# Another fixed instruction order for the engines of a hybrid SSM and attention layer, up to its first FFN tiles

## The chip, the cores and the metric

The kernel runs on one core of one Trainium2 chip. The time is the device time of one execution in microseconds; the time before is the median of three runs, 641.48 (640.93 to 643.57).

## What is computed

One layer of a hybrid encoder runs over 512 prompt tokens and 64 sample tokens (a running stream with 256 past keys), all in float32. Cut to what matters:

```python
def hybrid_layer(x, ckv_past, krope_past, ssm_h0, conv_buf, p):
    proj = rmsnorm(x, p['norm_mix']) @ p['w_in']        # z, xbc, dt, cq, ckv
    xbc, conv_new = causal_conv(xbc, conv_buf, p['conv_w'], p['conv_b'])
    dt = softplus(dt_raw + p['dt_bias'])
    y, h_new = ssd_scan(xh, dt, A, Bm, Cm, ssm_h0)      # chunks of tokens
    y_ssd = rmsnorm((y + d_skip * xh) * silu(z), p['ssd_norm'])
    q = rmsnorm(cq, p['q_norm']) @ p['w_uq']            # 8 heads: 64 + 32 rotary
    o = attention(q, keys)                              # mask in chunks of 64
    x = x + concat([y_ssd, o], -1) @ p['w_out']
    hf = rmsnorm(x, p['norm_ffn'])
    x = x + (silu(hf @ p['w_gate']) * (hf @ p['w_up'])) @ p['w_down']
```

A final norm follows. The new keys, the SSM state and the conv state are outputs too.

## The kernel before

The 576 tokens stand along the free axis, in two halves of 288; channels stand on the partitions in tiles of 128. A large product keeps its precision by splitting: a weight tile arrives by a DMA on SyncE's queue (`weights`, L119, 128 x 1024 floats, 512 KB, into one of seven slots of a pool), ScalarE casts it to its high part (L112, `wh_`) and VectorE subtracts to get the low part (L113, `wl_`). The operands are split in the same way (L142 on ScalarE, L144 or L146 on VectorE). Every product is then three passes, high by high, high by low, low by high (L128, and L443 for one half of the tokens at a time).

The stages, in the order in which the program is written:

- First: the first products (L128, `ps_first`, weights loaded at L213 and split at L217 and L218), their norms, and the small product `ps_small` (L292). The latter writes two 48-row results into two halves of the array's columns.
- Conv tiles 0 to 7 (`conv_tile`): a product into `ps_in` (L128, two PSUM buffers), its evacuation to `up` on VectorE (L382 to L384), the four-tap convolution (L389 on ScalarE, L391 three times on VectorE), a tanh (L393) and the result (L395, L396) into `xsd` or `bc`. Between them lies the step-size chain on VectorE (`sp_a`, L348 to L353), a run of small operations of 128 x 40, which starts from a transposition into `ps_dt` (L335).
- The rotary queries (`q_rope`): `ps_qr` (L128), then products with cosine and sine on VectorE (L421, L422 and L423, tiles `rrp` and `qt`). The PSUM pools of these stages are then closed, and their banks go to the next stages.
- z tiles (`ps_z`, L443, evacuated at L453), and the SSD scan in five chunks: `chunk_a` turns x and B (`ps_x` L483, `ps_b` L491), `chunk_e` builds the decays E (L506 to L514), `chunk_b` makes the outputs (`ps_y`, L527, and `ps_i`, L538), `chunk_s` the state (`ps_s`, L548), `gate` the gating and its norm (L567 to L573, `ps_g` L572).
- Values of the latent keys (`ps_v`, L590), and for each of four head pairs p: `pair_proj` (`ps_q` and `ps_k`, L443), scores of four query blocks and of the sample tokens (`sc` L657, `sc_s` L663), the softmax (`pr`, L640 to L647), turning (`ptp` L679, `ptp_s` L687), values (`pv` L704, and `pvs` L715 for the sample tokens), and splitting of the result (`cat`, L696 and L697).
- The output product in tiles of its own (`ps_o`, L443), then the FFN: `ps_p`, `ps_x`, `ps_y` and `ps_z` (L852), and `ps_d` (L988 and L1050).

Five of these matmuls fill only half of the array's columns, because their output has 48 or 64 rows for each head or half: L292, L527, L663, L704 and L715. Two that stand side by side write the two halves of one bank. This is L704's loop (L527 and L715 look alike):

```python
    for b in range(4):
        for j in range(2):
            h = 2 * p + j
            pe.matmul(
                pv[64 * j : 64 * j + 64, b * P :], V[b][:, h * HD : (h + 1) * HD], pts[p, b, j],
                start=b == 0, stop=True, skip_group_check=b > 0,
            )
```

The order of each engine's instructions is not the order of the program. After all of it is written, `issue_in_order` (L1296) takes, engine by engine, the list `ISSUE` of places: number n stands for the n-th instruction that the program gave this engine. Each instruction gets a dependency on the one ahead of it in the list, so each engine issues in just this order. The five lists are those of TensorE (PE), VectorE (DVE), ScalarE (ACT), GpSimd (POOL) and SyncE (SP); SyncE's and GpSimd's hold the DMAs that they issue.

Of the kernel before, what the change touches and what calls it, by code (L numbers as in the profile page):

```python
# [1295 lines left out]
def issue_in_order(tc, nc):  # L1296
# [13 lines left out]
0-7 20-21 8 14-16 9-13 22-25 38-41 17-19 32-36 26-31 42-43 56-59 37 50-55 68-69 44-47 60-61 74-79 92 48-49 62-67 80-85  # L1310
98-99 93-97 70-73 86-91 104-106 100-103 110 107-109 122-126 134-135 111-115 128-133 148-153 116-121 136-141 127
142-147 154-169 174-175 170-171 270-274 176-221 172-173 222-269 275-370 373-420 371 421-468 372 469-634 637 641-644
638-640 657-660 635-636 665-697 661 698-718 662 737-758 719-720 663-664 721-726 763 645-652 759-760 727-736 764-766
653-656 767-768 771-794 769-770 795-818 859 761-762 819-826 860-861 833-836 862-864 837-840 827-832 865-870 841-845
871-872 846-852 873-874 853-856 875-877 880 878-879 857-858 881-887 904-911 888 912 892-899 889-891 900-903 925-926
913-921 927-935 922-924 939-940 936-938 949-957 964-966 941 945-948 967 958-963 968-969 942-944 970-975 987 976-979
1003 980-986 991-993 988 1004-1005 1015-1021 1006-1014 1022-1024 994-996 1025-1026 1029-1034 1043-1045 997-998 989
1000-1002 999 1046-1054 990 1035-1039 1059-1061 1040-1042 1062-1064 1027-1028 1075-1077 1081-1092 1055-1056 1078-1080
1057 1093-1096 1058 1097-1104 1121-1123 1071-1072 1124-1129 1065 1068-1070 1073 1105-1107 1066-1067 1074 1130-1143
1119 1144-1156 1120 1229-1232 1157 1108-1112 1233-1240 1113-1114 1158 1241-1245 1115-1118 1159-1161 1246-1247 1176  # L1320
1253-1262 1177 1248-1252 1263-1264 1162-1175 1180 1178 1181-1182 1265 1183 1266-1268 1277-1278 1179 1279 1184-1187
1190-1195 1269-1275 1196-1204 1188-1189 1205-1223 1276 1227-1228 1224-1226 1280-1297 1301-1303 1298-1300 1304-1321
1342-1343 1348-1355 1344-1347 1322-1341 1356-1511 1572 1512-1559 1575-1576 1560-1571 1577 1596-1598 1578 1573-1574
1593 1584-1585 1579 1581-1583 1602-1604 1623-1625 1594-1595 1614 1586 1605-1606 1590-1592 1611-1613 1632-1634
1587-1589 1608-1610 1607 1580 1599-1601 1620-1622 1641 1626-1628 1647-1648 1629-1631 1649 1642-1643 1615-1616
1635-1637 1617-1619 1638-1640 1653 1656 1658-1667 1644-1646 1650-1652 1654-1655 1668-1669 1657 1682 1694-1705
1683-1693 1670-1681 1730-1741 1706-1729 1742-1748 1754-1755 1749-1753 1756-1767 1778-1785 1768-1777 1786-1885
1898-1905 1886-1897 1906-2017 2030-2036 2018-2029 2037-2053 2066-2084 2054-2065 2085-2089 2102-2104 2090-2101
2105-2221 2234-2236 2240-2241 2222-2233 2237 2242-2248 2238-2239 2249-2725 2738-2740 2744 2726-2737 2741 2745-2751
2742-2743 2752-3229 3242-3244 3248 3230-3241 3245 3249-3255 3246-3247 3256-3733 3746-3748 3752 3734-3745 3749  # L1330
3753-3759 3750-3751 3760-4189
""",
    "DVE": """
1 0 2-3 48 4-5 7 6 9 12 8 10-11 13-15 17 16 18-20 23 21-22 49 24 58 25 30 26 85 27-29 31-34 67-68 106 36 69 108 37 105
35 38 107 70 44 94 71 39 109 72-73 40-41 74 50-52 110 42 75 82 112 53 43 54-55 59-61 76 121 45 77-79 62 80 63-64 86-88
81 57 65 56 89 66 83 90 130 91 95 84 96-97 46 98-100 113-114 103 115 47 139 116 93 117 92 111 118 122-123 148 124
101-102 125 120 126-127 119 131-133 155 134 129 135-136 140-142 149 152 128 170 143-144 138 104 150 145 153 147 151
154 156 137 146 174 157 178 159 171-172 187 169 160 158 161-162 176 206 163 175 183 180 164 167 165-166 168 215 181
177 188 173 189 182 184 190 195 191 179 192-194 197 185-186 224 196 204 207-209 198-203 214 205 210 288 211 225
216-218 212 220 222 219 213 226 221 223 227-228 233 229 234 230-232 235-236 245 255 246 237 294 256 247 239 248 257  # L1340
259 258 260 240 238 264 241 261 242 263 262 307 267 243 265 244 266 274 249 268 270 251 269 253 250 252 254 275-276
289 271 290 277-279 295 286 280 282 281 287 272 297 317 291 283 318 273 298 302 299 316 300 284-285 319 303 306
292-293 296 309 312 304 326 305 310 308 313 327 362 311 328 322 301 323 314 363 330 324 320 329 315 336 321 325 364
333 367 337 331-332 365 340 338 334-335 341 344 349 339 345 350 342 346 352 351 343 355 358 366 347 359 357 348 360
356 353 361 368 377 354 370-371 369 372 375-376 373-374 382 390 378 384 383 385-386 379 389 387 380 397 388 381 393
405 395 391 396 398 394 392 400 399 401 403 402 420 406 404 408 407 409 412 410 417 414 411 413 418 462 416 421 423
419 464 425 422 424 415 433 431 426 432 429 428 427 438 430 434 469 463 436 435 437 439 442 441 443 466 440 444 451
465 446 467-468 452-453 445 447 455 454 448 473 475 456 477 476 474 457 472 470 478 458-459 449-450 479 460 481 480
461 471 482 491 487 483 496-497 484 488 498-499 489 500-502 485-486 503 510 490 515-518 522 492 504 519 506 520 507
521 508 532-535 539 546 493-495 536 547-549 505 511-512 509 523 537 529-530 524-525 513-514 531 538 540 528 550 541  # L1350
566 526 542 527 551 543 545 552 544 567-568 553-554 569 555 574 570 556-559 561 575-576 560 565 577 562 578-581 571
582-583 572 563 590-591 584 592 585-586 564 598 573 599-600 593-594 587-588 601 589 603 602 595 604-607 596 610 597
608-609 620-623 611 627 612 624 613-614 625-626 619 634-636 628 637 617 638 618 629 616 615 630 641 639 631 640 633
632 654-656 642 657 643 662 658 644-647 649 663-664 648 653 665 650 666-669 659 670-671 660 651 678-679 672 680
673-674 652 686 661 687-688 681-682 675-676 689 677 691 690 683 692-695 684 698 685 696-697 708-711 699 715 700 712
701-702 713-714 707 722-724 716 725 705 726 706 717 704 703 718 729 727 719 728 721 720 742-744 730 745 731 750 746
732-735 737 751-752 736 741 753 738 754-757 747 758-759 748 739 766-767 760 768 761-762 740 774 749 775-776 769-770
763-764 777 765 779 778 771 780-783 772 786 773 784-785 796-799 787 803 788 800 789-790 801-802 795 810-812 804 813
793 814 794 805 792 791 806 817 815 807 816 809 808 830-832 818 833 819 839 834 820-823 825 840-841 824 829 842 826
843-846 835 847-848 836 827 855-856 849 857 850-851 828 864 837 865-866 858 838 859 852-853 867 854 869 868 860  # L1360
870-873 861 876 862 874 880 875 881-883 887 884 863 885 877 886 879 878 888-898
""",
    "ACT": """
0-5 8 6-7 10 9 13 11 14 12 15 17-18 16 21 19 24 20 23 40 22 25 44 26-27 51 28-33 48-49 55 34-35 37 36 59 50 41-42
38-39 63 43 45-47 52-53 67 54 56-57 71 58 60-61 75 62 64-66 76 68-70 72 91 73-74 93 78 87 77 80 103 81 89 83 115 85-86
102 84 82 99 97 79 96 88 98 101 100 95 90 125 104 92 110 108-109 155 114 94 106-107 112 121 113 111 141 116 162 105
117-118 135 126 136 133 127 139 134 123 120 119 138 128 137 140 129 122 142 130 124 149 145 148 131 209 132 144 147
153 151 150 146 157-158 156 143 154 159-161 152 163-164 211 169 171 170 165 167 179 185 168 180 173 186 174 172 175
188 166 189 176 226 177 191 178 192 187 181 194 193 190 182 199 195 183-184 198 200 196 212 207 214-215 201-202 218
208 203 216 233 217 197 204-205 210 213 225 219 232 220 239 206 222 241 223 221 240 228 242-243 224 270 234 229 227  # L1370
230 237 236 271 231 244 235 247 238 245 248-251 246 256 254 260 253 261 255 258 262 257 264 252 266 265 263 267-268
277 269 259 272-276 283 279-281 284 286 282 278 292 285 290 287 289 288 301 291 293 295 294 297 299 296 300 302-303
# [123 lines left out]
```

## Time and profile before

| | |
|---|---|
| median of 3 runs | 641.48 us (640.93 to 643.57) |
| the profiled execution | 639.76 us, of which the span of its instructions is 638.1 |
| granted TensorE clock | 0.998 |
| stages, as windows of the span (us) | conv tiles 16 to 85; q_rope, z and SSD 85 to 149; attention 149 to 222; output product and first FFN tiles 222 to 306; rest of the FFN and the end from 306 |

A row of the timeline reads: start in us, length in us, engine, line, operation, output and inputs, array rows by columns used, shape, count in the group; in brackets the idle time before it and who ended it. Consecutive matmuls overlap, since the next one begins while the one before drains, so the cost of one is read from start to start. A plain float32 matmul counts as two records in the trace (x2), an fp32r pass as one. In a windows row stand start and end, length, and then for PE, PEld (weight loads), DVE, ACT and POOL the busy us with the number of instructions, the granted clock, the DMA share and GB/s. Numbers behind a tile's name tell its copies apart, and the profile leaves them out.

### The profile page before, as it was taken

To read this page: it belongs to the slowest core of one execution; us is meant where nothing else is said; L and a number is where in the kernel's file an instruction comes from. 1 tells how busy PE (TensorE), PEld (TensorE's weight loads), DVE (VectorE), ACT (ScalarE), POOL (GpSimd) and SP (SyncE) were. 2 spreads that over 40 slices of the span, in tenths; PEclk is the share of its full clock that TensorE was granted. 3 is DMA by queue.
4 is the path that set the end of the run, shared out by engine and by line. 5 is a ranking of instruction groups with operands and counts; after the bars stand their busy time and mean duration, and the time that the engine had idled before them with its cause. 6 is when DMAs were issued, how large, how long until landed. Compare 5 with 4: busy or idle time off the path is not lost.

```text
span 638.1 us, 12090 instructions
## 1 busy us (share of the span) xinstructions
PE 627.0 (98%) x4635; PEld 598.9 (94%) x4635; DVE 543.5 (85%) x945; ACT 400.9 (63%) x768; POOL 110.4 (17%) x164
## 2 busy tenths in 40 slices
PE   9999999999999999999999999999999999999996
PEld 8899999986787799999999999999999999999995
DVE  6999986899876699999999888988899789986555
ACT  7645436778775567766566676566757665767364
POOL 1322103101010000001300330033103220323323
PEclk9999999999999999999999999999999999999999
DMA  9322366322231133235643986398737892589914
GB/s 320 130 61 71 97 158 159 108 80 60 87 123 61 56 111 102 89 116 183 239 141 101 205 185 153 82 186 194 169 100 156 197 206 100 101 211 258 259 27 148
DMA packets 39593, 89.19 MB, mean 140 GB/s; under 512 B 4570, under 2 KB 14312, under 8 KB 39280
## 3 DMA queue, kind: packets, MB, share of 16 engines
q1 hardware_dynamic: 26416, 63.12, 30.5%
q0 software_dynamic: 12400, 24.73, 20.9%
q8 instruction: 36, 0.59, 0.4%
q10 hardware_dynamic: 720, 0.57, 0.3%
q14 instruction: 21, 0.17, 0.1%
HBM read 62.74 MB, written 24.53 MB: 137 GB/s over the span
## 4 chain that ended last, share of the span: by engine, by line
PE 84%; DVE 3%; ACT 1%; issue 1%; POOL 1%; DMA 1%; POOLq 0%; DVEq 0%; ACTq 0%
PE ps_x L852 21%; PE ps_d L1050 14%; PE ps_z L852 11%; PE ps_o L443 8%; PE ps_y L852 5%; PE ps_in L128 4%; PE ps_z L443 3%; PE ps_l L988 3%; PE ps_d L988 2%; PE ps_p L852 2%; PE sc L657 2%; PE pv L704 2%; PE ptp L679 1%; PE ps_v L590 1%; PE ps_q L443 1%
## 5 line engine op out<-in xcount | busy, mean ns | idle before, releaser
L852 PE MATMUL ps_x<-xop,wh_gu_S 128*128 128x288 f32 x504 | 101.7, 295 | 0.0
L852 PEld LDWEIGHTS ps_x<-xop,wh_gu_S 128*128 128x128 f32 x504 | 80.7, 188 | 0.2
L852 PE MATMUL ps_x<-xop,wl_gu_S 128*128 128x288 f32 x252 | 74.0, 294 | 0.0
L113 DVE TENSOR_TENSOR wl_gu_S<-gu,wh_gu_S 128x1024 fp32r<-128x1024 f32 x44 | 53.4, 1221 | 10.3 <-ACT wh_gu_S L112 6.8
L1064 POOL DMA_DIRECT2D acc<-fz x32 | 27.9, 907 | 167.2 <-ACT fz L1061 138.3
L112 ACT CAST wh_gu_S<-gu 128x1024 fp32r<-128x1024 f32 x44 | 46.3, 1052 | 15.9 <-PE ps_y L852 8.2
L852 PEld LDWEIGHTS ps_x<-xop,wl_gu_S 128*128 128x128 f32 x252 | 47.3, 188 | 0.0
L128 PE MATMUL ps_in<-xs,wh_in 128*128 128x288 f32 x256 | 45.3, 298 | 0.8 <-DVE sp_a L351 0.6
L128 PEld LDWEIGHTS ps_in<-xs,wh_in 128*128 128x128 f32 x256 | 37.6, 189 | 1.9 <-issue 0.9
L852 PE MATMUL ps_z<-xop,gu_a 128*128 128x288 f32 x252 | 38.3, 295 | 0.0
L852 PEld LDWEIGHTS ps_z<-xop,gu_a 128*128 128x128 f32 x252 | 35.0, 188 | 0.0
L852 PE MATMUL ps_z<-xop,wh_gu_S 128*128 128x288 f32 x168 | 34.9, 297 | 0.0
L852 PE MATMUL ps_x<-xop,wh_gu_A 128*128 128x288 f32 x168 | 34.6, 297 | 0.0
L852 PE MATMUL ps_y<-xop,wh_gu_A 128*128 128x288 f32 x168 | 33.9, 294 | 0.0
L112 ACT CAST wh_gu_A<-gu 128x1024 fp32r<-128x1024 f32 x22 | 23.1, 1051 | 10.4 <-PE ps_x L852 7.0
L443 PE MATMUL ps_o<-cat_y,wh_out 128*128 128x288 f32 x128 | 29.3, 312 | 0.4 <-ACT cat_y L142 0.4
L113 DVE TENSOR_TENSOR wl_gu_A<-gu,wh_gu_A 128x1024 fp32r<-128x1024 f32 x22 | 26.8, 1220 | 1.4 <-ACT wh_gu_A L112 1.0
L852 PEld LDWEIGHTS ps_z<-xop,wh_gu_S 128*128 128x128 f32 x168 | 27.2, 189 | 0.3 <-ACT wh_gu_S L112 0.3
L128 PE MATMUL ps_in<-xs,wl_in 128*128 128x288 f32 x128 | 27.4, 296 | 0.0
L852 PEld LDWEIGHTS ps_x<-xop,wh_gu_A 128*128 128x128 f32 x168 | 27.2, 189 | 0.1
L852 PEld LDWEIGHTS ps_y<-xop,wh_gu_A 128*128 128x128 f32 x168 | 26.9, 188 | 0.0
L443 PE MATMUL ps_z<-xs,wh_z 128*128 128x288 f32 x128 | 26.4, 299 | 0.0
(384 smaller groups left out, 2012.0 us busy)
## 6 DMA issues: line engine op xcount, KB each, us to landing
gu<-in_w_gu SPq DMA_DIRECT2D x44, 512.0 KB, 5.3
wr_d<-in_w_down SPq DMA_DIRECT2D x18, 512.0 KB, 4.1
acc<-fz POOLq DMA_DIRECT2D x16, 288.0 KB, 6.6
acc<-da POOLq DMA_DIRECT2D x16, 288.0 KB, 7.8
acc<-dc POOLq DMA_DIRECT2D x16, 288.0 KB, 8.4
wr_in<-in_w_in SPq DMA_DIRECT2D x8, 512.0 KB, 3.8
wr_out<-in_w_out SPq DMA_DIRECT2D x8, 512.0 KB, 3.2
cumb<-cumD SPq DMA_DIRECT2D x5, 512.0 KB, 4.6
```

Of the source, the lines that this page charges most:

```text
L112: act.copy(hi, raw)
L113: dve.tensor_tensor(lo, raw, hi.bitcast(F32), ALU.subtract)
L128: pe.matmul(ps[:m, hf, :n], w, x[:, hf * n : (hf + 1) * n], start=start and k == 0 and i == 0, stop=stop and k == last and i == 2,)
L443: pe.matmul(ps[:, :n], w, x[:, cols], start=k == 0 and i == 0, stop=k == len(terms) - 1 and i == 2,)
L590: pe.matmul(ps[:n], l, r, start=j == 0, stop=j == 2)
L657: pe.matmul(s[:, :nk], qs[:, j, q0 : q0 + P], ks[:, j, :nk], start=True, stop=True)
L679: pe.transpose(pp[:, k : k + P], prs[p, i][:, j, b * P : b * P + P], ident)
L704: pe.matmul(pv[64 * j : 64 * j + 64, b * P :], V[b][:, h * HD : (h + 1) * HD], pts[p, b, j], start=b == 0, stop=True, skip_group_check=b > 0,)
L852: pe.matmul(ps, p, q, start=not onto and first and kp == kps[0] and j == 0, stop=onto or (last and kp == kps[-1] and j == 2), skip_group_c ...
L988: pe.matmul(ps, w, x[:, cols], start=first and k == 0 and i == 0, stop=last and k == len(terms) - 1 and i == 2,)
L1050: pe.matmul(ps, p, v, start=not onto and n == 0 and j == 0, stop=onto or (n == len(ks) - 1 and j == 2), skip_group_check=onto,)
L1064: pool.dma_start(out, src, accum_op=ALU.add)
```

## The change

All five lists of `ISSUE` are replaced by others. In every list the places are the same numbers, so no instruction is added, removed or given other operands. TensorE's list is the same as before from place 1922 on, which lies in the first FFN tiles.

```diff
 ISSUE = {
     "PE": """
-0-7 20-21 8 14-16 9-13 22-25 38-41 17-19 32-36 26-31 42-43 56-59 37 50-55 68-69 44-47 60-61 74-79 92 48-49 62-67 80-85
...
+0-7 20-21 8 14-16 9-10 22 11-13 23-25 38-39 26-31 17-19 32-33 40 34-36 41-43 56 37 50-55 44-45 57-61 68-69 46-49 62-65
...
```

The numbers tell a reader nothing, so here are three places as rows of the two orders. The first is on TensorE, where head pair 0's values are computed (L704 `pv`, L715 `pvs`), with the next pairs' `ps_q` and `ps_k` (L443) about them. Before, from the scores that stand ahead of the values:

```order
L657 MATMUL sc_1_1_2075<-ks_385,qs_384 128x256
L704 MATMUL pv_2172<-pt_0_2035,V_1659 64x512 x2
L704 MATMUL pv_2172<-pt_1_2098,V_1659 64x384 x2
L704 MATMUL pv_2172<-pt_2_2087,V_1670 64x256
L715 MATMUL pvs_2233<-pts_2052,V_1681 64x64 x3
L704 MATMUL pv_2172<-pt_2_2087,V_1670 64x256
L704 MATMUL pv_2172<-pt_2_2087,V_1670 64x128 x2
L715 MATMUL pvs_2233<-pts_2052,V_1681 64x64
L715 MATMUL pvs_2233<-pts_2052,V_1692 64x64 x2
L663 MATMUL sc_s<-ks_385,qs_384 64x320 x2
L443 MATMUL ps_q_0_2287<-cqn_481,wh_pair_2244 128x288 x2
L443 MATMUL ps_q_0_2287<-cqn_481,wl_pair_2245 128x288
```

And now, from the first of the values:

```order
L704 MATMUL pv_2172<-pt_0_2035,V_1659 64x512
L657 MATMUL sc_1_1_2075<-ks_385,qs_384 128x256
L704 MATMUL pv_2172<-pt_0_2035,V_1659 64x512
L704 MATMUL pv_2172<-pt_1_2098,V_1659 64x384
L663 MATMUL sc_s<-ks_385,qs_384 64x320
L715 MATMUL pvs_2233<-pts_2052,V_1681 64x64
L443 MATMUL ps_q_1_2196<-cqn_481,wh_pair_2155 128x288 x2
L443 MATMUL ps_q_1_2196<-cqn_481,wl_pair_2156 128x288
L443 MATMUL ps_q_1_2196<-cqn_484,wh_pair_2155 128x288 x2
L443 MATMUL ps_q_1_2196<-cqn_484,wl_pair_2156 128x288
L715 MATMUL pvs_2233<-pts_2052,V_1681 64x64 x3
L663 MATMUL sc_s<-ks_385,qs_384 64x320
```

What stood in one run behind each other, the eight values of the prompt, the sample's and the scores of the next sample block, is now dealt out among full-width products; the remaining values of this pair follow in the same manner, in four more pieces.

The second place is on VectorE, in the conv tiles: the step-size chain (`sp_a`, L350 to L353), the evacuations (L382 to L384), the weight splits (L113) and the copy of the keys (L313). Before:

```order
L384 TENSOR_TENSOR up_631<-ps_in_582,R_99 128x64
L350 SCALAR_TENSOR_TENSOR sp_a<-sp_a,sp_q 128x40
L113 TENSOR_TENSOR wl_in_914<-wr_in_911,wh_in_913 128x1024
L313 TENSOR_TENSOR ckv<-ckf,ckv 128x832
L350 SCALAR_TENSOR_TENSOR sp_a<-sp_a,sp_q 128x40 x3
L391 SCALAR_TENSOR_TENSOR cacc_639<-up_631,hcw,cacc_639 128x579
L350 SCALAR_TENSOR_TENSOR sp_a<-sp_a,sp_q 128x40
L391 SCALAR_TENSOR_TENSOR cacc_639<-up_631,hcw,cacc_639 128x579 x2
L382 TENSOR_TENSOR up_732<-ps_in_683,R_99 128x288
L383 TENSOR_TENSOR up_732<-ps_in_683,R_99 128x224
L384 TENSOR_TENSOR up_732<-ps_in_683,R_99 128x64
L351 SCALAR_TENSOR_TENSOR sp_a<-sp_a,sp_s 128x40
```

And now, up to the end of the chain:

```order
L352 TENSOR_SCALAR dt<-dt 128x40
L350 SCALAR_TENSOR_TENSOR sp_a<-sp_a,sp_q 128x40 x2
L391 SCALAR_TENSOR_TENSOR cacc_567<-up_559,hcw,cacc_567 128x579
L310 SCALAR_TENSOR_TENSOR ckf<-ckr,par,Rk 128x576
L391 SCALAR_TENSOR_TENSOR cacc_567<-up_559,hcw,cacc_567 128x579 x2
L382 TENSOR_TENSOR up_631<-ps_in_582,R_99 128x288
L383 TENSOR_TENSOR up_631<-ps_in_582,R_99 128x224
L384 TENSOR_TENSOR up_631<-ps_in_582,R_99 128x64
L396 SCALAR_TENSOR_TENSOR xsd<-cth_572,cacc_567 128x64
L395 SCALAR_TENSOR_TENSOR xsd<-cth_572,cacc_567 128x512
L351 SCALAR_TENSOR_TENSOR sp_a<-sp_a,sp_s 128x40
L353 SCALAR_TENSOR_TENSOR dt<-sp_a,dt 128x40
```

The chain is now at its end before the second evacuation's tile is convolved, and the split of `wr_in_914` and the copy L313 no longer stand between the chain's steps; they come later.

The third place is on VectorE at the rotary queries (L421 to L423). Before:

```order
L421 TENSOR_TENSOR rrp<-ps_qr_1133,cos_sin 128x576 x2
L395 SCALAR_TENSOR_TENSOR xsd<-cth_979,cacc_974 128x512
L113 TENSOR_TENSOR wl_z_1324<-wr_z_1321,wh_z_1323 128x1024
L391 SCALAR_TENSOR_TENSOR cacc_1118<-up_1110,hcw,cacc_1118 128x579 x2
L396 SCALAR_TENSOR_TENSOR bc<-cth_1051,cacc_1046 128x64
L362 TENSOR_SCALAR ncum<-ps_cum 128x40
L422 TENSOR_TENSOR qt_419<-ps_qr_1146,cos_sin 128x576
L391 SCALAR_TENSOR_TENSOR cacc_1118<-up_1110,hcw,cacc_1118 128x579
L422 TENSOR_TENSOR qt_420<-ps_qr_1146,cos_sin 128x576
L396 SCALAR_TENSOR_TENSOR bc<-cth_1123,cacc_1118 128x64
```

And now:

```order
L421 TENSOR_TENSOR rrp<-ps_qr_1133,cos_sin 128x576 x2
L391 SCALAR_TENSOR_TENSOR cacc_1118<-up_1110,hcw,cacc_1118 128x579
L422 TENSOR_TENSOR qt_419<-ps_qr_1146,cos_sin 128x576
L391 SCALAR_TENSOR_TENSOR cacc_1118<-up_1110,hcw,cacc_1118 128x579
L422 TENSOR_TENSOR qt_420<-ps_qr_1146,cos_sin 128x576
L391 SCALAR_TENSOR_TENSOR cacc_1118<-up_1110,hcw,cacc_1118 128x579
L423 TENSOR_TENSOR rrp<-rrp,qt_419 128x576
L423 TENSOR_TENSOR rrp<-rrp,qt_420 128x576
L396 SCALAR_TENSOR_TENSOR bc<-cth_1123,cacc_1118 128x64
L113 TENSOR_TENSOR wl_z_1324<-wr_z_1321,wh_z_1323 128x1024
```

The split of the z weights 1324 stood ahead of the L422 products; it now stands behind them and behind L423. SyncE's queue moves too: the first conv weights (`wr_in_504`) are now issued ahead of four of the eight first-product weights (L213), and the loads of the chunks' decays (L473, L479) and of `ks_385` (L603) change places with the z and pair weights.

More of the change, by code (lines that the diff above doesn't have):

```diff
@@ new lines @@
+391-420 371 421-468 372 469-500 517-520 501-507 521-522 508 523 509-516 524-595 613-617 596-608 618-621 637 641
+609-610 622-632 611-612 633-636 642 638-640 665-672 689-696 673-681 697-705 682-688 706-712 643-644 713-717 657 718
+737-752 658 753 659-662 645-647 754-755 653 756-757 648-649 719-725 654 726-727 758-759 650-651 760 652 728-736
+655-656 771-774 795-797 775-776 663 763-764 664 777-783 765-767 798-799 784-794 800-818 761-762 819-824 768-770
+825-826 833-835 859-860 836-839 861-864 840 827-832 865-867 841-842 845-854 868-872 880-881 873 855-856 843-844
@@ new lines @@
+1293-1296 1288 1297-1299 1301-1307 1300 1308-1329 1342 1330-1332 1348-1355 1333-1341 1356 1343-1347 1357-1377
+1380-1382 1378-1379 1383-1426 1428-1429 1427 1430-1504 1572 1505-1511 1575 1512-1515 1581 1516-1522 1578 1523
+1579-1580 1584-1585 1524-1547 1573-1574 1593 1548-1553 1599-1600 1554-1557 1560-1563 1558 1564-1566 1594 1567-1570
+1559 1571 1582-1583 1602 1595 1614 1601 1576-1577 1596-1597 1590 1587-1589 1620 1608-1609 1591-1592 1610 1629
+1615-1616 1635 1621 1586 1605-1607 1598 1617-1619 1603-1604 1623-1625 1644 1611-1612 1630 1613 1631 1650 1632-1634
@@ new lines @@
+1653 1638 1626 1636-1637 1622 1656 1639-1640 1658-1659 1651 1645-1646 1654 1627-1628 1647 1660-1662 1655 1663-1668
+1641-1643 1648-1649 1657 1682 1694-1705 1669 1683-1684 1652 1685-1693 1670-1680 1730-1732 1681 1733-1739 1706-1729
+1742-1750 1766-1767 1740-1741 1751 1778-1788 1752-1765 1768-1776 1790-1791 1777 1792-1813 1789 1826-1828 1832-1834
+1838-1840 1844-1846 1814-1825 1829-1831 1841-1842 1850-1852 1843 1853-1858 1862-1863 1868-1869 1864-1865 1870
+1835-1837 1847-1849 1859-1861 1866 1871-1872 1867 1874-1885 1898-1908 1886-1887 1909 1888-1897 1910-1921 1873
```

147 lines of the change are left out of this document (71 added, 76 removed).

## The prediction

> **What bounds the kernel now.** I read the page first: which engine is full, and which engine the last chain runs through. The third row gives the size and the landing time of one kind of weight load.
>
> ```profile
> PE 627.0 (98%) x4635; PEld 598.9 (94%) x4635; DVE 543.5 (85%) x945; ACT 400.9 (63%) x768; POOL 110.4 (17%) x164
> ...
> PE 84%; DVE 3%; ACT 1%; issue 1%; POOL 1%; DMA 1%; POOLq 0%; DVEq 0%; ACTq 0%
> ...
> wr_in<-in_w_in SPq DMA_DIRECT2D x8, 512.0 KB, 3.8
> ```
>
> TensorE is busy for 98% of 638.1 us, so all waits together hold about 11 us, start and end included. A new order gains only what it takes out of those waits, and loses whatever it makes TensorE itself do more slowly. The second view is the list of TensorE's waits (total, times, longest).
>
> ```profile
> PE sc L657 <- ACT pr L641: 1.1, 2, 0.9
> ...
> PE ps_x L483 <- DVE qt L422: 0.8, 1, 0.8
> PE ps_in L128 <- DVE sp_a L351: 0.6, 1, 0.6
> ...
> PE ps_o L443 <- ACT cat_y L142: 0.4, 1, 0.4
> ...
> PE ps_in L128 <- DVE sp_a L350: 0.2, 1, 0.2
> ```
>
> These five lie ahead of the first FFN tiles, where the change is. The third view is the windows: busy time of PE, PEld, DVE, ACT, POOL in each stretch, then the granted clock.
>
> ```profile
> 149.00:160.00 11.00, 9.64 (x48) 6.26 (x47) 10.76 (x32) 10.68 (x35) 1.95 (x4) 1.00 0.29 86
> 254.00:306.00 52.00, 52.00 (x388) 51.28 (x387) 51.25 (x84) 34.00 (x58) 2.74 (x5) 1.00 0.40 132
> 222.00:306.00 84.00, 84.00 (x626) 83.01 (x626) 81.72 (x139) 56.18 (x92) 2.74 (x5) 1.00 0.38 125
> 306.00:638.00 332.00, 325.77 (x2452) 325.02 (x2451) 279.02 (x433) 206.66 (x365) 75.75 (x91) 1.00 0.67 162
> ...
> 160.00:222.00 62.00, 61.45 (x443) 48.88 (x442) 43.85 (x106) 40.29 (x110) 1.91 (x4) 1.00 0.21 75
> ```
>
> Attention (160 to 222) is TensorE's alone: 61.45 of 62 us. Where attention starts (149 to 160) VectorE and ScalarE are full and TensorE waits. From 222 on, TensorE and VectorE are nearly full together. The clock is 1.00 everywhere, so no term for it is needed. The busy number hides one thing, and it is the main term: weight loads (PEld) run beside matmuls at 83.01 of 84 in the FFN's stretch, but only at 48.88 of 62 in attention.
>
> **Part 1: what the new order adds on TensorE.** No instruction is added. But matmuls that fill half of the array's columns (tile 128*64 at L292, L527, L663, L704 and L715) stand closer or farther apart. I call one run of them between full-width matmuls a visit. Two visits of before, with their neighbours:
>
> ```profile
> 142.20 0.29 PE L443 MATMUL ps_q<-cqn,wl_pair 128*128 128x288 f32 x1
> 142.43 1.09 PE L527 MATMUL ps_y<-E,xdt 128*64 128x128 f32 x16
> 143.45 0.49 PE L538 MATMUL ps_i<-bc,h 128*128 128x128 f32 x2
> 143.69 0.63 PE L443 MATMUL ps_k<-ckv,wh_pair 128*128 128x416 f32 x2
> 144.16 0.35 PE L443 MATMUL ps_k<-ckv,wl_pair 128*128 128x416 f32 x1
> 144.35 1.02 PE L548 MATMUL ps_s<-xw,bt 128*128 128x256 f32 x4
> 145.21 0.38 PE L538 MATMUL ps_i<-bc,h 128*128 128x128 f32 x2
> ...
> 181.52 0.35 PE L443 MATMUL ps_k<-ckv,wl_pair 128*128 128x416 f32 x1
> 181.80 0.76 PE L663 MATMUL sc_s<-ks,qs 100*64 100x320 f32 x4
> 182.49 0.54 PE L443 MATMUL ps_q<-cqn,wh_pair 128*128 128x288 f32 x2
> 182.86 0.29 PE L443 MATMUL ps_q<-cqn,wl_pair 128*128 128x288 f32 x1
> ```
>
> Matmuls overlap, so I count from start to start. L548 does 1024 columns in 145.21 - 144.35 = 0.86 us: 0.84 ns per column. The L443 pass over 416 columns takes 144.35 - 144.16 = 0.19. A 288-column pass takes 0.1325 (four from 50.71 to 51.24, quoted below). Two halves of a pair run side by side, since 16 passes of L527 last only 143.45 - 142.43 = 1.02. The second visit's work is then 0.19 + 2 x 320 x 0.84 ns = 0.54 + 2 x 0.1325 = 0.27, together 1.00; from 181.52 to 182.86 are 1.34. The first one's work is 0.13 + 8 x 0.1075 = 0.86 + 2 x 0.1075 = 0.22 + 0.38, together 1.59; from 142.20 to 144.16 are 1.96. A visit costs 0.34 and 0.37 beyond its work: I take **0.35 us**, whatever its length.
>
> In TensorE's order I count 13 visits before and 30 after: the small product 1 to 2; the SSD chunks' ps_y 6 to 10 (its first chunk alone 1 to 4); the sample scores of head pairs 0 and 2 that stand alone, 1 each in both; the values of pair 0, 1 to 7; of pair 1, 1 to 4; of pair 2, 1 to 2; of pair 3, 1 to 3. So 17 x 0.35 = 5.95 us; **6.0**.
>
> Splitting also parts pairs. What a half costs without its partner:
>
> ```profile
> 130.10 1.09 PE L527 MATMUL ps_y<-E,xdt 128*64 128x128 f32 x14
> 131.12 0.68 PE L590 MATMUL ps_v<-wh_uv,ckv 128*64 128x512 f32 x2
> ```
>
> Here 14 passes last 1.02 us, as long as the 16 above, so a lone half takes the time of a pair. For pair 0's values, each matmul passes twice, so a 512-column step takes 2 x 512 x 0.84 ns = 0.86, and 384, 320, 256 and 128 take 0.65, 0.54, 0.43 and 0.22. Before: 0.86 + 0.65 + 0.43 + 0.22, sample values 0.2, sample scores 0.54: 2.9. After, in seven visits: 0.86 (a lone 512), 1.2 (512 beside 384, then a lone 320), 0.54, 1.08 (384 then 256, one half), and 0.22, 0.22, 0.1: 4.2. That is +1.3; the other visits add about 0.2. **1.5**, between 0.8 (neighbours of other kinds pair up after all) and 2.0.
>
> Added: 6.0 + 1.5 = **7.5 us**, between 17 x 0.30 + 0.8 = 5.9 and 17 x 0.37 + 2.0 = 8.3. It lies on TensorE's own path, where nothing covers it.
>
> The Trainium skill, page "TensorEngine Tiling (Array Packing)", section "Key Properties", has a rule of the same sign: "Changing tiling mode (not just tile) drains the TensorE". It gives no price; the two rows above do.
>
> **Part 2: what the new order takes away.** The two waits in the conv tiles, and a row that stands for a few small ones (38.52):
>
> ```profile
> 50.71 0.69 PE L128 MATMUL ps_in<-xs,wh_in 128*128 128x288 f32 x4
> 51.24 0.43 PE L128 MATMUL ps_in<-xs,wl_in 128*128 128x288 f32 x2
> 51.89 0.78 PE L128 MATMUL ps_in<-xs,wh_in 128*128 128x288 f32 x4 [0.22 <-DVE sp_a L350]
> ...
> 58.08 0.43 PE L128 MATMUL ps_in<-xs,wl_in 128*128 128x288 f32 x2
> 59.14 0.76 PE L128 MATMUL ps_in<-xs,wh_in 128*128 128x288 f32 x4 [0.63 <-DVE sp_a L351]
> ...
> 38.52 0.90 PE L128 MATMUL ps_in<-xs,wh_in 128*128 128x288 f32 x4
> 39.26 0.43 PE L128 MATMUL ps_in<-xs,wl_in 128*128 128x288 f32 x2
> ```
>
> Two passes need 0.27; they take 0.65 and 1.06, so 0.38 + 0.79 = **1.2** is lost. What TensorE waits for is the conv tile's evacuation (L382 to L384), queued on VectorE behind weight splits, the ckv copy and the step-size chain. In the new order the ckv copy and two splits stand behind it: I take all 1.2 as gone, bound 0.4 (only the first). At 38.52, 0.74 stands where four passes need 0.53: **0.2**, bound 0.
>
> ```profile
> 94.49 0.29 PE L443 MATMUL ps_z<-xs,wh_z 128*128 128x288 f32 x1
> 95.58 0.27 PE L483 MATMUL ps_x<-ident,xsd 128*64 128x128 f32 x1 [0.80 <-DVE qt L422]
> ...
> 90.31 1.22 DVE L113 TENSOR_TENSOR wl_z<-wr_z,wh_z 128x1024 fp32r<-128x1024 f32 x1 [1.40 <-ACT wh_z L112]
> ```
>
> 1.09 for one pass of 0.13: **1.0** lost. VectorE stood 1.40 us before the split wl_z, and the rotary products (L422) that free the bank were queued behind it. The new order puts this split after them. Late next is the split itself, needed only by the third z tile; bound 0.3.
>
> Attention's start: 11.00 - 9.64 = 1.36 idle, and 0.4 at ps_o, so 1.8 at most. ScalarE's 10.68 and VectorE's 10.76 us of work there must still be done. I take **1.2**: TensorE's sample values and scores now fill holes there, bounds 0 and 1.8.
>
> Towards the FFN: 52.00 us for 388 matmuls is 0.1340 each, against 325.77 / 2452 = 0.1329 later: 0.43 lost to a VectorE at 51.25 of 52. A TensorE that arrives later finds its splits ready: **0.4**, bound 0. Gains: 1.2 + 0.2 + 1.0 + 1.2 + 0.4 = **4.0 us**, between 0.7 and 4.6 (and 1.5 more if waits too short for these rows go too).
>
> SyncE's queue: a 512 KB conv weight now goes ahead of four first-product weights.
>
> ```profile
> L213 SPq DMA_DIRECT2D wr_first<-in_w_first x8: 328/424/432, 1.3 to 9.9; - x8
> ...
> L217 ACT CAST wh_first<-wr_first x7: 494/509/515, 6.8 to 17.8; 128x384 fp32r<-128x384 f32 x7
> ...
> DMA to landing us min/median/max: 3.0/4.8/5.4
> ```
>
> The last was issued at 9.9, so it landed by 15.3, and its cast began at 17.8: 2.5 us of cover against a landing of 3.8. I cost it at 0, with 3.8 - 2.5 = 1.3 as its price without luck. GpSimd's moves are clears and small copies on an engine 17% busy: 0.
>
> **Sum.** 7.5 - 4.0 = +3.5 us. On the profiled execution: 639.76 + 3.5 = 643.3. That execution lies 1.7 below the median of the runs, 641.48; on the median the sum is 645.0. I give **644.8**, since the short waits not counted can only take from it. The ends: 5.9 - (4.6 + 1.5) = -0.2 gives 641.3; 8.3 - 2.0 (half of the gains; their low ends together are the first rival's case) = +6.3 gives 647.8.
>
> **The rivals.**
> - *The waits stay* (0.20). VectorE is 81.72 of 84 us busy near the FFN and ScalarE is full at 149 to 160; moved work may stand before another evacuation. Then only the conv and z waits, 1.2 or 1.0, go: +7.5 - 1.2 = +6.3 to +6.5, **648**. It decides if any evacuation of L382 to L384 again starts over 0.3 us after its product. Against it: the places where these splits stood are clear ones.
> - *The visits fall into waits* (0.14). Visits placed where TensorE waits for ScalarE anyway cost nothing there. For it: 149 to 160 is 1.36 us idle. Against it: by the order, at most four of the 17 new visits stand there, the rest in stretches 98% busy or more. Four visits less, 1.4, and 1.5 of short waits: +0.6, **642.1**.
> - *The visits cost nothing* (0.06), the other side: their price is a wait of weight loads, and in mixed order they are loaded in advance. Then +1.5 - 4.0 = -2.5, **639.0**. Against it stands this row of PEld:
>
> ```profile
> 181.80 0.20 PEld L663 LDWEIGHTS sc_s<-ks,qs 100*64 100x64 f32 x4 [0.28 <-issue]
> ```
>
> The load begins with its matmul at 181.80, after 0.28 in which nothing was waited for, though the matmul before had begun at 181.52. It wasn't taken in advance.
>
> The Trainium skill, page "TensorE: Matmul & The Clock Gate" (its table at the top), says that TensorE's queue "pulls LDWEIGHTS ahead of in-flight MATMULs"; by this rule the visits would be free, which is this rival. At a visit's entry the row does not show it.
>
> **How the numbers follow.** My forecast, +1 to +5.5, has 0.60; the rivals 0.20, 0.14 and 0.06. A measurement of this kernel tells about 0.5%, 3.2 us, from no change: that parts the forecast at +3.2, half to each side. Slower by more: 0.30 + 0.20 = 0.50; faster: 0.05; the same: 0.45. The range runs from 640.8, which leaves out most of the third rival, to 648.2, the middle of the first.
>
> **What the new profile would show.** The waits list loses both sp_a rows and the qt row. The visits' stretch, 160 to 222, grows by over 5 us at no more wait. The first FFN matmul of low weights (L852 ps_p with wl_gu_S) starts 2 to 5 us later, and from there the trace runs as before. A visit would again show about 0.35. The prediction is wrong if a visit of few matmuls costs less than 0.2, or if waits of over 0.5 us stand at new places.

## The result, and the profile after

The changed kernel takes 647.41 us (median; 647.07 to 647.95, 4 runs) against 641.43 for the kernel before in the same comparison: the ratio is 1.0088, 95% interval 1.0063 to 1.0112, so it is slower, by 4.0 to 7.2 us. The profiled execution took 647.07 us, its span is 645.4 against 638.1. The forecast was slower at 644.8, range 640.8 to 648.2.

The page of the changed kernel, first its busy times:

```profile
span 645.4 us, 12089 instructions
...
PE 633.2 (98%) x4635; PEld 600.0 (93%) x4635; DVE 546.0 (85%) x945; ACT 400.5 (62%) x768; POOL 115.5 (18%) x164
```

TensorE does the same 4635 records and is busy for 6.2 us longer (633.2 against 627.0); VectorE and GpSimd do the same instructions in 2.5 and 5.1 us more. So the loss is not only idle time: the same instructions last longer on three engines.

Two marks that both orders pass after the same TensorE work divide the loss. The first is the first z pass (620 records lie ahead of it in both), the second the first pass of the FFN's `ps_z` with the weights `gu_a` (1931 records lie ahead of it before, 1930 now). The list of the new order joins the old one only some 30 us behind this second mark; the row's last pass tells whether anything is added there. Of the kernel before, the timeline row and the row of the tile's list (duration min/median/max, first to last start):

```profile
88.46 0.37 PE L443 MATMUL ps_z<-xs,wh_z 128*128 128x288 f32 x1
...
L852 PE MATMUL ps_z<-xop,gu_a x252: 288/294/310, 272.2 to 601.5; 128*128 128x288 f32 x126
```

And of the changed kernel:

```profile
91.66 0.37 PE L443 MATMUL ps_z<-xs,wh_z 128*128 128x288 f32 x1 [0.25 <-DVE rrp L421]
...
L852 PE MATMUL ps_z<-xop,gu_a x252: 288/294/310, 279.4 to 608.8; 128*128 128x288 f32 x126
```

Up to the z tiles 3.2 us are lost (88.46 to 91.66), from there to the FFN 4.0 more (7.2 at 279.4), and behind it nothing (7.3 at 608.8). The forecast had about -1 for the first stretch and about +4.5 for the second. So the second came nearly as worked out, and the first with the wrong sign. Together they are 7.2 us in these two executions, against 3.5 in the forecast's sum. TensorE's waits in the changed kernel:

```profile
PE ps_in L128 <- DVE wl_in L113: 1.1, 1, 1.1
...
PE ps_qr L128 <- DVE up L384: 1.1, 1, 1.1
PE ps_in L128 <- DVE up L384: 0.8, 1, 0.8
PE ptp L679 <- DVE pr L647: 0.8, 1, 0.8
...
PE sc_s L663 <- ACT pr L641: 0.4, 1, 0.4
...
PE ps_z L443 <- DVE rrp L421: 0.2, 1, 0.2
```

The rows of sp_a and qt are gone, as forecast, but three new ones on VectorE stand in their place: 3.0 us instead of 1.6. What makes VectorE late is seen when its timeline is laid beside GpSimd's. VectorE's rows of the changed kernel:

```profile
43.30 1.60 DVE L177 TENSOR_TENSOR nr_u<-nr_u,nr_v 128x576 f32<-128x576 f32 x1
...
46.28 0.21 DVE L384 TENSOR_TENSOR up<-ps_in,R 128x64 f32<-128x64 f32 x1
46.41 1.70 DVE L350 SCALAR_TENSOR_TENSOR sp_a<-sp_a,sp_q 128x40 f32<-128x40 f32 x3
...
62.73 2.02 DVE L404 TENSOR_TENSOR kr<-kr,kt 16x576 f32<-16x576 f32 x1
64.68 0.44 DVE L382 TENSOR_TENSOR up<-ps_in,R 128x288 f32<-128x288 f32 x1
```

And GpSimd's at the same times:

```profile
43.14 1.16 POOL L241 TENSOR_SCALAR_AFFINE_SELECT qs<-qs 4x1152 f32<-4x1152 f32 x1
...
46.01 1.58 POOL L241 TENSOR_SCALAR_AFFINE_SELECT ks<-ks 4x1664 f32<-4x1664 f32 x1
...
62.27 1.88 POOL L241 TENSOR_SCALAR_AFFINE_SELECT ks<-ks 4x1664 f32<-4x1664 f32 x1
```

L241 builds a mask for the rotary keys and queries on four partitions, and needs SBUF for over 1 us. Each of the three VectorE instructions begins while one runs and ends shortly after it: L404 would last 0.74, but from 62.73 it ends at 64.75, 0.60 after L241's end at 64.15. In the kernel before, the four L241 ran from 27 to 32 us; there VectorE was reading PSUM (L254, L261 and L300), and nothing was held up. Their first and last row before:

```profile
27.02 1.21 POOL L241 TENSOR_SCALAR_AFFINE_SELECT qs<-qs 4x1152 f32<-4x1152 f32 x1
...
30.83 1.58 POOL L241 TENSOR_SCALAR_AFFINE_SELECT ks<-ks 4x1664 f32<-4x1664 f32 x1
```

In the changed kernel, the evacuations (L382 to L384) for which TensorE waits at 46.63 stand close behind L177 on VectorE, and those behind L404 stand ahead of the weight split for which it waits at 68.07.

The visits are as they were read from the kernel before. Head pair 0's values in the changed kernel:

```profile
172.37 0.35 PE L443 MATMUL ps_k<-ckv,wl_pair 128*128 128x416 f32 x1
172.65 1.07 PE L704 MATMUL pv<-pt,V 128*64 128x512 f32 x2
173.66 0.70 PE L657 MATMUL sc<-ks,qs 100*128 100x256 f32 x2
174.28 1.07 PE L704 MATMUL pv<-pt,V 128*64 128x512 f32 x4
```

From 172.37 to 174.28 are 1.91 us, for work of 0.19 (416 columns) + 0.86 (a lone half, two passes of 512) + 0.43 (two of 256), together 1.48: 0.43, of which the next visit's entry is a part. PEld is idle at its edge again: the load of the first `pv` begins at 172.65 with its matmul, after 0.28 us in which nothing was waited for. Over 160 to 222 its busy time falls from 48.88 to 44.94 us:

```profile
160.00:222.00 62.00, 61.17 (x388) 44.94 (x387) 41.94 (x105) 40.47 (x111) 3.98 (x8) 1.00 0.18 59
```

TensorE looks as busy as before (61.17 against 61.45) and gets through 388 records instead of 443. The two windows do not hold the same matmuls, so this is a sign of the loss and not its measure; the marks give that.

### The profile page after: what moved, and what is told of

Its sections match the earlier page's. It is cut to its first block, busy times and chain, and to the rows that moved or that the text cites. A ratio compares the mean times of both kernels' runs of the same rounds, so it can differ in the third digit from the quotient of the medians.

```text
span 645.4 us, 12089 instructions
## 1 busy us (share of the span) xinstructions
PE 633.2 (98%) x4635; PEld 600.0 (93%) x4635; DVE 546.0 (85%) x945; ACT 400.5 (62%) x768; POOL 115.5 (18%) x164
## 4 chain that ended last, share of the span: by engine, by line
PE 89%; DVE 6%; issue 2%; ACT 1%; POOL 1%; DMA 1%; POOLq 0%; ACTq 0%; DVEq 0%
PE ps_x L852 21%; PE ps_d L1050 14%; PE ps_z L852 10%; PE ps_o L443 8%; PE ps_y L852 5%; PE ps_z L443 4%; PE ps_in L128 3%; PE ps_first L128 3%; PE ps_l L988 3%; PE sc L657 2%; PE ps_d L988 2%; PE pv L704 2%; PE ps_p L852 2%; PE ptp L679 1%; DVE cacc L391 1%
## 5 line engine op out<-in xcount | busy, mean ns | idle before, releaser
L113 DVE TENSOR_TENSOR wl_gu_S<-gu,wh_gu_S 128x1024 fp32r<-128x1024 f32 x44 | 53.4, 1222 | 10.2 <-ACT wh_gu_S L112 6.9
L443 PE MATMUL ps_o<-cat_y,wh_out 128*128 128x288 f32 x128 | 29.1, 315 | 0.0
L113 DVE TENSOR_TENSOR wl_gu_A<-gu,wh_gu_A 128x1024 fp32r<-128x1024 f32 x22 | 26.8, 1220 | 1.5 <-ACT wh_gu_A L112 1.3
L1009 POOL DMA_DIRECT2D acc<-dn x8 | 4.4, 547 | 128.1 <-ACT dn L1008 128.1
L443 PE MATMUL ps_z<-xs,wh_z 128*128 128x288 f32 x128 | 26.7, 302 | 0.2 <-DVE rrp L421 0.2
```

The source lines that it names most:

```text
L113: dve.tensor_tensor(lo, raw, hi.bitcast(F32), ALU.subtract)
L443: pe.matmul(ps[:, :n], w, x[:, cols], start=k == 0 and i == 0, stop=k == len(terms) - 1 and i == 2,)
```

## The experiments

Each run has its ratio to the kernel before, measured on the same chip. To compare with the changed kernel I use its 1.0088. The times in the expectations stand on the first comparison (641.48 before, 647.4 changed), so a ratio times 641.48 is what compares with them.

**1. The masks early, alone.** In GpSimd's list:

```diff
 L93 MEMSET ones 128x128
+L239 MEMSET qs_382 4x1152
+L239 MEMSET ks_383 4x1664
 L336 MEMSET dt 128x40
+L406 DMA krall<-in_cache_kropeT 32x256
+L241 AFFINE_SELECT (all four)
...
-L239, L241 between the conv tiles' clears
```

> The changed kernel with one list altered, GpSimd's: the six instructions that build the rotary masks (L239, L241) go back to the early place that they have in the kernel before. Theory 1 (GpSimd's long mask instructions hold up VectorE's instructions with two SBUF inputs: in the changed kernel L177 at 43.30 took 1.60 us for 0.76, L350 at 46.41 1.24 for 0.20, L404 at 62.73 2.02 for 0.74, each while an L241 ran): the three go back to their usual lengths, VectorE gains 0.85 + 1.05 + 1.29 = 3.2 us by 65 us, TensorE's waits at 46.63 (0.84) and 68.07 (1.13) go; 645.4 to 646.2. Theory 2 (VectorE's own new order is too late at these places, whatever GpSimd does): the waits stay or come back within 20 us, 647.0 to 647.6.

The load L406, which only issues a DMA, moves along with the masks. In the changed kernel it is issued at 67.48, after the three held-up instructions, so it can't be what held them up.

Measured: 644.78 us, 1.0062 (1.0041 to 1.0082), about 2 us less. This interval and the changed kernel's overlap, so the time alone would not prove the gain; the trace and run 6 do. The held-up instructions have their length again (rows of VectorE, in this run):

```profile
43.77 0.76 DVE L177 TENSOR_TENSOR nr_u<-nr_u,nr_v 128x576 f32<-128x576 f32 x1
...
46.03 0.66 DVE L350 SCALAR_TENSOR_TENSOR sp_a<-sp_a,sp_q 128x40 f32<-128x40 f32 x3
...
61.37 0.75 DVE L404 TENSOR_TENSOR kr<-kr,kt 16x576 f32<-16x576 f32 x1
```

Both ps_in waits are gone from TensorE's list, and the wait at the rotary queries is down to 0.3:

```profile
PE ps_qr L128 <- DVE up L384: 0.3, 1, 0.3
```

Theory 1 stands. The first z pass comes at 89.02 instead of 91.66, 2.6 us earlier.

**2. The visits put together, alone.** In TensorE's list of the changed kernel, the pieces of a run are put together, at several places; for instance

```diff
-L704 pv 512 | L657 | L704 pv 512, 384, L663, L715 | L443 x6 | L715 x3, L663 | L443 x6 | L704 384, 256 x2
+L657 | L443 x12 | L704 pv 512 x2, 384 x2, 256 x2, L715 x4, L663 x2
```

> The changed kernel with TensorE's list altered: 30 visits of half-width matmuls are put together to 19 (ps_small 2 to 1, ps_y of chunks 0 and 3 by 1 each, head pair 0's values 7 to 2, pair 1's 4 to 2, pair 2's with its sample scores 2 to 1), and halves that stood alone are paired again. Theory of the prediction (0.35 us a visit, a lone half costs as much as a pair): 11 x 0.35 + 1.3 = 5.1 us less, 642.0 to 643.0, unless a delayed result makes a new wait. Rival A (only parted pairs cost, not the visits): 1.3 less, about 646.1. Rival B (neither costs; the time lies in waits elsewhere): 647.0 to 647.8.

Measured: 646.71 us, 1.0091 (1.0068 to 1.0114): nothing gained. By time alone that is rival B. TensorE's waits say more:

```profile
PE ps_q L443 <- ACT ks L611: 1.3, 1, 1.3
...
PE sc_s L663 <- ACT pr L641: 1.1, 2, 0.6
...
PE ps_g L572 <- ACT ysq L569: 0.8, 1, 0.8
...
PE ps_o L443 <- DVE wl_out L113: 0.5, 1, 0.5
...
PE ps_o L443 <- DVE qs L607: 0.4, 1, 0.4
```

Four of these are new, 3.0 us, and sc_s is 0.7 longer: 3.7 of the 5.1 that were expected to be gained. At the longest, TensorE now comes to `ps_q` before ScalarE has got to the copy L611, which it runs at nearly its old time (175.85, against 175.44 in the changed kernel). Elsewhere ScalarE is late because the halves themselves come later: its softmax of the sample scores (L641) runs at 181.19 instead of 178.84. Another 0.7 us is a new wait for the weights of the first products. So in the changed kernel's lists the pieces partly stand in for waiting. Whether the visits cost anything had to be tested where the other engines' lists don't hang on the pieces.

**3 and 4. The kernel before with one run dealt out.** In its TensorE list, the 16 half-width matmuls of head pair 0 (one visit) are dealt among the 18 full-width passes behind them, in 7 visits: with the pairs whole, then in the changed kernel's order, which parts them.

```diff
 L704 pv 64x512 x2
-L704, L715, L663 (14)
 L443 x3
+L704 pv 64x384 x2, L663 64x320 x2
 L443 x3
+L704 pv 64x256 x2
...
```

> The kernel before with TensorE's list altered at one place: the run of 16 half-width matmuls of head pair 0's values is dealt out among the 18 full-width passes that follow it, in 7 visits of whole pairs. Theory (0.35 us a visit): 6 x 0.35 = 2.1 more, 643.0 to 643.7, and in the trace the stretch from the first of the 16 to the last of the 18 grows by 1.8 to 2.3 us without a wait. Rival (a visit is free): 641.2 to 641.7, stretch the same.

> As the run before, but the 16 matmuls are dealt in the order and the 7 groups (1, 4, 4, 3, 2, 1, 1) of the changed kernel, which parts the pairs. Theory (0.35 us a visit, and a lone half costs as much as a pair): 2.1 + 1.3 = 3.4 more, 644.4 to 645.1. Rival (a lone half costs its half only): as with whole pairs, 643.0 to 643.7. Rival (visits free): 641.2 to 642.8.

Measured: 642.53 us, 1.0035 (1.0022 to 1.0049), and 644.28, 1.0055 (1.0036 to 1.0075). A clean visit with a whole pair, in the first of the two:

```profile
177.71 0.29 PE L443 MATMUL ps_o<-cat_y,wl_out 128*128 128x288 f32 x1
177.94 0.65 PE L704 MATMUL pv<-pt,V 128*64 128x256 f32 x4
178.52 0.53 PE L443 MATMUL ps_o<-cat_y,wh_out 128*128 128x288 f32 x2
178.89 0.29 PE L443 MATMUL ps_o<-cat_y,wl_out 128*128 128x288 f32 x1
```

1.18 us from 177.71 to 178.89, for 0.13 + 0.43 + 0.27 = 0.83: 0.35 again. And the first visit of each run, a whole pair in the first and a lone half in the second:

```profile
174.00 1.08 PE L704 MATMUL pv<-pt,V 128*64 128x512 f32 x4
175.41 0.54 PE L443 MATMUL ps_q<-cqn,wh_pair 128*128 128x288 f32 x2 [0.33 <-DVE qs L607]
...
171.70 1.07 PE L704 MATMUL pv<-pt,V 128*64 128x512 f32 x2
173.11 0.53 PE L443 MATMUL ps_q<-cqn,wh_pair 128*128 128x288 f32 x2 [0.34 <-DVE qs L607]
```

Without the wait the pair takes 1.08 us (1.41 - 0.33) and the lone half 1.07 (1.41 - 0.34).

The whole stretch, from the first `pv` to the scores behind it, took 8.11 us before (170.99 to 179.10). It takes 9.88 with whole pairs (174.00 to 183.87), 0.33 of it a wait that is new, and 11.76 with parted ones (171.70 to 183.47), with the same wait. So dealing out costs 1.44 for six visits more, 0.24 each: less than 0.35, and less than the 1.8 to 2.3 us expected for the stretch. A likely reason is that the one long visit pays inside it too, where it changes from `pv` to `pvs` and back: there TensorE takes 3.91 us (170.99 to 174.90) for the 2.9 of work that the prediction counts. Parting the pairs costs 1.89 more, against 1.3 worked out. The ratios give 643.7 and 645.0 on the expectations' scale, both within the theory's ranges. Both free-visit rivals fall, and that of a half that costs half. (The first run's stretch begins 3 us late, behind windows with a granted clock of 0.93 and 0.97; in the stretch the clock is 1.00.)

**5 and 6. The later stages as before.** In the changed kernel, the instructions from the first z tile on stand among each other as in the kernel before, on all five engines; then with early masks as well.

```diff
 (all five lists)
-from the first z tile on: the new relative order
+from the first z tile on: the relative order of the kernel before
+(second run) GpSimd: L239, L241 as in the run with early masks
```

> The changed kernel, in which all instructions that the program writes from the first z tile on (z, SSD, attention, output product, FFN) stand among each other, on all five engines, as in the kernel before; the stages up to the rotary queries keep the new order. 14 visits of half-width matmuls instead of 30, and no engine's order in the later part is fitted to dealt-out pieces. Theory (the visits and parted pairs cost 6.0 + 1.5 us, and the run with merged visits kept its time only because ScalarE's and VectorE's queues of the new order then came late): 16 x 0.35 + 1.5 = 7.1 less than the changed kernel's 647.4, the waits at the start of attention 0.6 longer: 640.3 to 641.5. Rival (the visits fill time in which TensorE would wait for ScalarE and VectorE in any order): as with merged visits, 645.5 to 647.0.

> The same, with GpSimd's mask instructions (L239, L241) at their early place as well. Theory: 2.2 less again, as in the run with early masks alone: 638.2 to 639.3, under the kernel before. Rival (TensorE then waits for VectorE or ScalarE elsewhere before 149 us): 640.0 to 641.0.

Measured: 642.52 us, 1.0023 (1.0012 to 1.0034), and 639.42, 0.9977 (0.9966 to 0.9988). The first takes 0.0065 of the ratio away, about 4.2 us; its rival falls. In the trace TensorE takes 182.8 us between the two marks, against 187.7 in the changed kernel and 183.8 in the kernel before. The later stages' loss belongs to their order, and it does not come back as waits when all engines' lists fit together. But the 640.3 to 641.5 of the theory is not reached: 4.2 to 4.9 us come back where the theory had 7.1, less 0.6 of waits. The second run takes another 0.0046 away, about 3 us, by GpSimd's list alone, and here the two intervals lie clear of each other. It beats the kernel before by about 1.5 us; its time is missed with that of the first run, on which it stood (640.0 on the expectations' scale, where the rival begins; but no new wait of over 0.3 us stands in TensorE's list). Its first z pass and its last mark, where the kernel before has 88.46 and 272.2:

```profile
88.62 0.37 PE L443 MATMUL ps_z<-xs,wh_z 128*128 128x288 f32 x1 [0.24 <-DVE rrp L421]
...
L852 PE MATMUL ps_z<-xop,gu_a x252: 288/294/310, 271.6 to 600.8; 128*128 128x288 f32 x126
```

The new front part without its masks is no faster than the old one (88.62). What is gained comes behind it: the wait for qt, 1.0 us, is gone from TensorE's list.

**7. The front part in the kernel before.**

```diff
 (all five lists of the kernel before)
-ahead of the first z tile: its own relative order
+ahead of the first z tile: the new relative order, late masks
```

> The kernel before, in which the instructions that the program writes ahead of the first z tile (first products, conv tiles, step sizes, rotary queries, masks) stand among each other as in the changed kernel, on all five engines. It has the late masks. Theory (masks cost about 2.2 us, the order of VectorE saves 1.2 in the conv tiles, ps_small's second visit costs 0.35): 641.9 to 642.9. Rival (the front part of the change saves as was predicted, its masks cost nothing): 639.8 to 640.3.

Measured: 646.71 us, 1.0099 (1.0072 to 1.0125), far above both expectations. The run does not isolate what it was meant to: the front instructions fill places that the old list left for others, and TensorE waits for the rotary products at the first z pass.

```profile
PE ps_z L443 <- DVE rrp L421: 2.5, 1, 2.5
PE ps_qr L128 <- DVE up L384: 1.2, 1, 1.2
```

It shows only how little an order's parts can be exchanged at a seam.

**8. The z weights' split later, alone,** in the kernel before:

```diff
-L113 wl_z_1324
 L391 x2, L396, L362, L422, L391, L422, L396, L423 x2
+L113 wl_z_1324
```

> The kernel before with one instruction of VectorE moved: the split of the z weights 1324 (L113) stands behind the rotary products (L422, L423) instead of ahead of them. Theory: TensorE's wait for qt before the transpositions of x (1.0 us at 95.58) goes, nothing else comes late: 639.9 to 640.4. Rival (the split is then late for its z tile, or TensorE waits for ScalarE next): 640.8 to 641.6.

Measured: 642.15 us, 1.0020 (1.0009 to 1.0032): slightly slower, above even the rival's range. In the profiled execution 0.76 us of this stands ahead of the first z pass (89.22 instead of 88.46), where the edit changes nothing: a conv weight was waited for longer there (ScalarE 1.78 us, before 0.70). VectorE now waits at the next instruction, and longer (2.30 against 1.40), for ScalarE:

```profile
91.97 0.82 DVE L391 SCALAR_TENSOR_TENSOR cacc<-up,hcw,cacc 128x579 f32<-128x579 f32 x1 [2.30 <-ACT cacc L389]
```

and ScalarE has the cast of the same weights ahead of that L389, waiting for their DMA:

```profile
90.11 1.05 ACT L112 CAST wh_z<-wr_z 128x1024 fp32r<-128x1024 f32 x1 [3.22 <-DMA wr_z<-in_w_in]
91.07 0.87 ACT L389 ACTIVATE cacc<-up,hcw 128x579 f32<-128x579 f32 x1
```

So the stall at qt had two queues in it, not one: the load's landing held ScalarE, and through it VectorE. Moving the split on VectorE alone frees little (0.56 us of the wait of 0.80 are left), and a later z pass waits instead (0.87 us at 99.25, put down to ScalarE's el, which is queued behind the next z cast).

**9. Late masks in the kernel before.** Only GpSimd's list is altered (the copies L245 of the masks move along):

```diff
-L239 x2, L336, L406, L241 x4
+L336, L406, L239, L241, ... L380, L239, L241, ... L380, L241, ... L380, L241
```

> The kernel before with GpSimd's list alone altered: the masks' instructions (L239, L241) stand between the clears and copies of the conv tiles, at the neighbours that they have in the changed kernel. Theory (a mask instruction holds up VectorE's two-input instructions in the conv tiles): single VectorE instructions of 45 to 65 us are 0.8 to 1.6 longer, TensorE's waits in the conv tiles grow by 1 to 3 us together, 641.8 to 643.8. Rival (the loss belongs to the changed kernel's VectorE order, and early masks only happened to suit it): 640.4 to 641.0.

Measured: 640.16 us, 0.9986 (0.9977 to 0.9995): no loss, rather a small gain. By the time alone the rival would have it. But the holding up is there, on other instructions. VectorE's and, last, GpSimd's rows:

```profile
48.22 2.31 DVE L309 TENSOR_TENSOR cq<-cq,Rq 128x1152 f32<-128x1152 f32 x1
...
52.04 0.45 DVE L382 TENSOR_TENSOR up<-ps_in,R 128x288 f32<-128x288 f32 x1
...
52.84 0.78 DVE L350 SCALAR_TENSOR_TENSOR sp_a<-sp_a,sp_q 128x40 f32<-128x40 f32 x1
...
61.75 1.61 DVE L396 SCALAR_TENSOR_TENSOR bc<-cth,cacc 128x64 f32<-128x64 f32 x1
...
51.55 2.02 POOL L241 TENSOR_SCALAR_AFFINE_SELECT ks<-ks 4x1664 f32<-4x1664 f32 x1
```

L309 takes 1.35 and L396 0.22 without a mask beside them. Beside the L241 of 51.55, which ends at 53.57, the evacuation L382, which reads PSUM, keeps its 0.45, while L350, with two inputs in SBUF, takes 0.78 instead of 0.19 and ends at 53.62. But the qt row has left TensorE's list: the first z pass is 1.4 us later than before (89.83), the second mark only 0.4 (272.6). What came late in the conv tiles was made up at the wait for the z weights, which were underway in the meantime. So the mechanism holds and its price does not carry over: it is paid only if no later wait absorbs it. Why the median is even lower, this run doesn't settle.

**10. The small product once more in one visit,** in the fastest version:

```diff
-L292 x2 | L128 x5 | L292 x14
+L128 x5 | L292 x16
```

> The fastest version so far (new order up to the rotary queries, early masks, order of the kernel before from the first z tile on) with ps_small's two visits put together to one. Theory (a visit costs 0.24 to 0.35 us): 0.2 to 0.4 less than that version's 1.2 under the kernel before, so 1.4 to 1.6 under it. Rival (the two matmuls that stood ahead filled a gap of the first products): the same as that version, 1.2 under the kernel before, or slower.

Measured: 639.01 us, 0.9976 (0.9965 to 0.9986): the two versions' intervals lie over each other, so 0.3 us can't be seen in the times. It is the fastest version of the study, about 1.5 us under the kernel before.

## Why the prediction came as it did, point by point

- **Slower, by TensorE's own work: right for the later stages,** 4.0 of the 7.2 us between the profiled executions. The price of a visit was read as 0.35 us; the clean one of run 3 is 0.35. As a net price of dealing out a run it is 0.24. The price of parted pairs was put too low: 1.89 against 1.3 at one place. Between the marks, the later stages lost 4.0 us where the terms (16 visits there, 1.5 for pairs, less 1.0, 1.2 and 0.4) gave about 4.5; taking their order back won about 4.2.
- **The time: within the range, and partly by luck.** The measured 647.41 is 2.6 above the forecast. The 3.2 us of the front part come from a place where the forecast had a gain of about 1; the range reached so far for other reasons (dearer visits, fewer gains).
- **"I take all 1.2 as gone" (conv waits): wrong.** The old rows did go, but 1.9 us of new ones stand in the same tiles. Run 1 shows their cause, the masks.
- **"GpSimd's moves are clears and small copies on an engine 17% busy: 0": wrong, and this is the step that failed most.** Among the moved instructions are the four L241, 1.2 to 1.9 us each. They cost about 2 us (run 1), or about 3 (between runs 5 and 6, 0.0046 of the ratio). I looked at what GpSimd was waited for, not at whom it holds up by running.
- **The wait at qt, 1.0: right that it goes, wrong why.** The split ahead of L422 was only one of two queues (run 8). The new order also puts ScalarE's L389 ahead of its cast of the z weights: in run 6 the cast comes as late as before (89.30, before 89.23), but L389 at 87.22, and VectorE's L391 at 88.39 waits for nothing.
- **Attention's start, 1.2: not seen as such.** The sc rows (1.1) are replaced by ptp 0.8 and 0.2 more at sc_s; 0.5 is left of the gain at most by these rows.
- **SyncE's queue at 0: not contradicted.** TensorE waits for no first weights in the changed kernel's list; in runs 1, 2, 5 and 6, which have the new order there, rows of 0.2 to 0.7 stand for them, so the cover is thinner than 2.5 us.
- **The signs named ahead: two came, others did not.** The sp_a and qt rows left the list, and a visit shows 0.35 again. But waits of over 0.5 us stand at new places (0.84, 1.13, 1.09 and 0.8), which the prediction itself named as a sign of being wrong, and rightly so: they are the step above on GpSimd, and attention's start. The later stages grew by 4.0 between the marks and not by over 5. The first `ps_p` pass with `wl_gu_S` starts 9.0 us later (253.9, now 262.9) and not 2 to 5; the new order moves it among the FFN's own passes, so it was no good mark.
- **The rivals.** "The waits stay", at 648, is nearest to the measured 647.41, and its mechanism, another instruction ahead of an evacuation, did happen, but by GpSimd and not by VectorE's order. "The visits fall into waits" is partly true within the changed kernel's own lists (run 2), but it doesn't make them free (runs 3 to 5). "The visits cost nothing" is excluded.

What stays open: how the later stages' 4 us divide between visits, parted pairs and saved waits, since these exchange with each other when only one engine's list is changed (run 2).

## What to carry to other kernels

Whoever prices an order by adding up measured durations treats a duration as a property of the instruction; here a matmul's depended on the tile shape of its neighbours, and a VectorE instruction's on what GpSimd ran beside it. So before pricing a reordering, group instructions by the resource that they share (array tiling, SBUF access), and count the changes of group, not the instructions. And price an engine that nobody waits for by what it slows while it runs; then test one engine's list against the others', for lists that were fitted together can't be judged alone.

## What the runs showed of the hardware

- An affine select on four partitions on GpSimd held up VectorE instructions with two SBUF inputs for up to its whole length: three L350 took 1.70 instead of 0.66, L404 2.02 instead of 0.74, L396 1.61 instead of 0.22 us, while instructions with one input from PSUM beside them were not lengthened (L382 0.45 beside one, L261 and L300 the same 1.41 and 1.88 in the kernel before, beside one, as in the changed kernel without). The Trainium skill says so on the page "SBUF — State Buffer", section "SBUF: two separate sides": the pair of SBUF ports that VectorE and GpSimd share is an exclusive lock, held for a whole instruction, on which the other fully blocks; it counts among these a VectorE instruction with two SBUF inputs against a GpSimd one that reads SBUF. The traces agree, with L404's end 0.60 us after L241's.
- A lone half-width matmul takes the time of a pair (1.07 and 1.08 us over 512 columns), and a change of tile shape at the array costs about 0.35 us there and back, whatever stands between (three clean visits: 0.34, 0.37 and 0.35).
